# Attention of a two-layer decoder: the negative maximum and first exponential of a row group ahead of the filling work, one score chunk in a transposition bank, and a head's reciprocals turned one block later

## The chip, the cores and the metric

The kernel runs on one core of a Trainium2 chip. The metric is the device time of one execution in microseconds (us), and lower is better. Every time below is in us unless ns is written.

## The reference

The program is a two-layer decoder trunk on 2048 tokens of width 1024: a Mamba-2 layer, then multi-head latent attention whose keys and values come from a shared latent, then a final RMS norm. The change touches the attention alone. It has 16 heads, queries and keys of 64 + 32 channels, values of 64, and a causal mask:

```python
def causal_block_attention(q_nope, q_rope, k_nope, k_rope, v):
    for i in range(S // Q_BLOCK):
        ...
        s = (q_nope @ k_nope + q_rope @ k_rope) * scale
        p = softmax(where(mask, s, -inf))
        outs.append(p @ v[:, :kv_len])
```

The softmax's division is done later here: the exponentials go into the product with v undivided, their row sums are kept, and the reciprocals multiply the gate in the last stage (`back`).

## The kernel before

**Stages.** `mamba`, `mla` (projections), `heads` (attention, from about 2008 us of the profiled execution to 2908) and `back` (output projection, gate, norm). Only `heads` is written differently after the change.

**Tiling of the attention.** For each of 16 heads there are four query blocks (0 to 3) of 512 rows, each of four row groups of 128 rows. The scores of a row group are cut into chunks of at most 512 keys: one chunk in block 0, two in block 1, three in block 2, four in block 3 (`cuts`). In this text

- **S b.j.n** is the score chunk n of row group j in block b: three matmuls (lines 88 to 90), and for the group's last chunk a fourth that adds the mask (L1220). It fills one PSUM bank. The banks are eight: four with the tag `mm`, four with the tag `tr`. Scores take `mm` banks in rotation, so that the fifth chunk waits until the first one's exponential has read its bank.
- **M b.j.n** is the row maximum of the chunk, a reduction on VectorE (L1221), **N b.j** the negative maximum over the group's chunks, `nm` (L1225, VectorE), and **E b.j.n** the exponential on ScalarE (L1233), which needs N b.j, writes `Pr` and sums its rows into `sm`. L1237 reduces `sm` into the head's `sums`.
- **T b.k** turns key tile k of a block's exponentials: up to four transpositions (L1248) into one `tr` bank. **H b.k** (ScalarE, L119) and then **L b.k** (VectorE, L120) split the bank into two f16 halves `PTs`; after L the bank is free. **V b.k** multiplies both halves with the values (L1258, L1259) into the block's accumulator, which holds another `tr` bank during the block and is read by `Os` (ScalarE, L1265).
- **R** is the transposition of a head's 16 reciprocals (L1277); `rT` (ScalarE, L1279) reads it.

**Order.** TensorE's order is written out by hand. `scores` is a generator that yields after each chunk a word of T's and V's from the table `CREDIT`; the loop then issues that many turnings and products of blocks that are 20 chunks behind. This is the filling work: beside a head's block 2 the turnings of the head before's block 3 and of its own block 0 are issued, beside its block 3 those of its own blocks 1 and 2. In block 3 the last chunk of row group 0 is followed by `VVTTVTV`. The order of ScalarE and VectorE is made by a scheduler from the order in which the code emits its instructions. On all three engines it is the same in each head from 2 to 13, before the change and after it.

In the code before, the exponentials of a row group are put in a list `late` when the generator is called again, that is behind the filling work of the group's last chunk, and are issued one a chunk ahead of the next group's chunks:

```python
                    yield CREDIT[qb][j][n]
                nm = self.t(sp, "nm", [P, 1], bufs=4)
                v.tensor_reduce(nm, mx[:, :nb], AX.X, ALU.max, negate=True)
                ...
                late += [lambda n=n, f=exp: f(n) for n in range(nb)]
```

Queues: TensorE, ScalarE and VectorE each work in order. SyncE issues the stores of `Os` and `rT` and the loads of the output weights, GpSimd the other half of the stores and the loads of keys, values and queries. The loads of the output weights begin in head 13, and in heads 14 and 15 ScalarE converts them (`W<-wr` and `K<-wr`, L1331) between its attention work.

Of the kernel before, what the change touches and what calls it, by code (L numbers as in the profile page):

```python
# [21 lines left out]
P = 128  # L22
# [15 lines left out]
NP = 24  # L38
# [33 lines left out]
class Net:  # L72
# [1108 lines left out]
    def heads(self, sp):  # L1181
        nc, v = self.nc, self.nc.vector
        begun = []
        keys, vals, quer = self.keys, self.vals, self.quer

        def cuts(kv):

            out, at = [], 0
            while at < kv:
                w = min(TB, kv - at)  # L1190
                if kv - at == TB + P:
                    w = 384
                out.append((at, w))
                at += w
            return out

        def scores(h, qb, st):

            if h + 1 < NH:
                if qb == 2:  # L1200
                    self.load_k(h + 1, 0, NB)
                    self.load_v(h + 1)
                self.load_q(h + 1, qb)
            Q, K = quer.pop((h, qb)), keys[h]
            late = []
            for j in range(4):
                qs = slice(j * P, (j + 1) * P)
                parts = cuts(qb * TB + (j + 1) * P)
                nb = len(parts)
                mx = self.t(sp, "mx", [P, 4], bufs=4)  # L1210
                banks = []
                for n, (c0, w) in enumerate(parts):
                    if late:
                        late.pop(0)()
                    begun.append(0)
                    s = self.t(self.pp, "tr" if len(begun) <= 18 and len(begun) % 2 == 1 else "mm", [P, TB], bufs=4)
# [4 lines left out]
                    v.tensor_reduce(mx[:, n:n + 1], s[:, :w], AX.X, ALU.max)  # L1221
                    banks.append((s, w))
                    yield CREDIT[qb][j][n]
                nm = self.t(sp, "nm", [P, 1], bufs=4)
                v.tensor_reduce(nm, mx[:, :nb], AX.X, ALU.max, negate=True)  # L1225
                p = {}
                sm = self.t(sp, "sm", [P, 4], bufs=4)
                st["P"].append(p)

                def exp(n, j=j, nb=nb, parts=parts, banks=banks, nm=nm, p=p, sm=sm):  # L1230
                    s, w = banks[n]
                    x = self.t(sp, "Pr", [P, TB], bufs=NP)
                    nc.scalar.activation(x[:, :w], s[:, :w], AF.Exp, bias=nm, accum_out=sm[:, n:n + 1])  # L1233
                    for c in range(0, w, P):
                        p[(parts[n][0] + c) // P] = x[:, c:c + P]
                    if n == nb - 1:
                        v.tensor_reduce(sums[h][:, 4 * qb + j:4 * qb + j + 1], sm[:, :nb], AX.X, ALU.add)  # L1237

                late += [lambda n=n, f=exp: f(n) for n in range(nb)]
            for f in late:  # L1240
                f()

        def turn(h, qb, kb, st):

            jj = max(kb - 4 * qb, 0)
            pt = self.t(self.pp, "tr", [P, TB], bufs=4)
            for j in range(jj, 4):
                nc.tensor.transpose(pt[:, j * P:(j + 1) * P], st["P"][j][kb], self.ident)  # L1248
            c = slice(jj * P, TB)
            u = self.t(sp, "PTs", [P, 2, TB], F16, bufs=5)  # L1250
            self.pair16(u[:, 0, c], u[:, 1, c], pt[:, c], PSCALE)
            return u[:, :, c], c

        def values(h, qb, kb, st, u, c):
            if kb == 0:
                st["O"] = self.t(self.pp, "tr", [P, TB], bufs=4)
            nk = 4 * qb + 4
            nc.tensor.matmul(st["O"][:, c], vals[h][:, kb, :], u[:, 0], start=kb == 0, stop=False)  # L1258
            nc.tensor.matmul(st["O"][:, c], vals[h][:, kb, :], u[:, 1], start=False, stop=kb == nk - 1)  # L1259
            if kb == nk - 1:  # L1260
                finish(h, qb, st)

        def finish(h, qb, st):
            o = self.t(sp, "Os", [P, TB], bufs=3)
            nc.scalar.activation(o, st["O"], AF.Copy)  # L1265
# [36 lines left out]

        step = 0
# [206 lines left out]
```

## Time and profile before

| what | us |
|---|---|
| median of 3 runs (lowest, highest) | 3099.84 (3098.41, 3102.62) |
| the profiled execution's own time | 3099.32 |
| its span | 3097.2 |
| TensorE, VectorE, ScalarE, GpSimd busy | 2994.5, 2330.1, 1936.4, 615.3 |
| granted TensorE clock, mean | 0.995 of full speed |

The profile is of one execution, and the span is what its instructions cover. "Busy" of TensorE is from modelled ends: a 512-wide f16 matmul shows 0.38, while in a dense stretch the next one starts 0.216 after it, so matmuls overlap in the rows and a short wait between two of them is hidden by the overlap. Waits of TensorE are therefore counted below from start to start: what the distance exceeds the same distance in a dense stretch.

### The profile page before, as it was taken

To read this page: it belongs to the slowest core of one execution; us is meant where nothing else is said; L and a number is where in the kernel's file an instruction comes from. 1 tells how busy PE (TensorE), PEld (TensorE's weight loads), DVE (VectorE), ACT (ScalarE), POOL (GpSimd) and SP (SyncE) were. 2 spreads that over 40 slices of the span, in tenths; PEclk is the share of its full clock that TensorE was granted. 3 is DMA by queue.
4 is the path that set the end of the run, shared out by engine and by line. 5 is a ranking of instruction groups with operands and counts; after the bars stand their busy time and mean duration, and the time that the engine had idled before them with its cause. 6 is when DMAs were issued, how large, how long until landed. Compare 5 with 4: busy or idle time off the path is not lost.

```text
span 3097.2 us, 51355 instructions
## 1 busy us (share of the span) xinstructions
PE 2994.5 (97%) x17758; PEld 1759.2 (57%) x17758; DVE 2330.1 (75%) x5306; ACT 1936.4 (63%) x4920; POOL 615.3 (20%) x842
## 2 busy tenths in 40 slices
PE   7899999999999999999999999999999999999998
PEld 3466655555455554545555555456666666665777
DVE  7789887777777687797755453488888888888576
ACT  8777566665667656565534333388888888888422
POOL 0211122211222112222111212322122222222100
PEclk9999999999999999999999999999999999999999
DMA  8675436445454466364466555622223222232485
GB/s 298 221 235 181 151 106 220 129 158 163 153 191 162 131 207 222 121 199 145 145 214 197 194 173 170 197 49 60 55 56 67 54 58 57 54 88 75 130 261 158
DMA packets 205065, 457.11 MB, mean 148 GB/s; under 512 B 28114, under 2 KB 57554, under 8 KB 203364
## 3 DMA queue, kind: packets, MB, share of 16 engines
q1 hardware_dynamic: 176948, 375.94, 37.9%
q0 software_dynamic: 27856, 77.89, 9.8%
q8 instruction: 140, 2.29, 0.3%
q14 instruction: 121, 0.99, 0.1%
HBM read 340.99 MB, written 112.73 MB: 146 GB/s over the span
## 4 chain that ended last, share of the span: by engine, by line
PE 40%; DVE 5%; ACT 4%; issue 3%; DMA 2%; POOL 0%; SPq 0%; ACTq 0%; POOLq 0%; DVEq 0%
PE mm L88 7%; PE mm L90 6%; PE mm L89 6%; PE tr L1248 6%; PE tr L1259 3%; PE tr L1258 3%; PE tr L88 3%; PE tr L90 3%; PE tr L89 3%; ACT Pr L1233 2%; DVE PTs L120 1%; DMA os<-ri_d 1%; ACT PTs L119 1%; DVE mx L1221 1%; PE mm L1220 0%
## 5 line engine op out<-in xcount | busy, mean ns | idle before, releaser
L120 DVE SCALAR_TENSOR_TENSOR PTs<-tr,PTs 128x512 f16<-128x512 f32 (+3 forms) x640 | 374.2, 606 | 76.8 <-ACT PTs L119 69.7
L1233 ACT ACTIVATE Pr<-mm,nm 128x512 f32<-128x512 f32 (+2 forms) x631 | 394.2, 635 | 49.4 <-DVE nm L1225 44.9
L1221 DVE TENSOR_REDUCE mx<-mm 128x1 f32<-128x512 f32 (+2 forms) x631 | 373.1, 604 | 31.1 <-PE mm L90 28.3
L119 ACT ACTIVATE PTs<-tr 128x512 f16<-128x512 f32 (+3 forms) x640 | 329.4, 544 | 97.9 <-PE tr L1248 95.9
L1248 PE MATMUL tr<-pack,Pr 128*128 128x128 f32 x2176 | 317.5, 273 | 1.8 <-ACT Os L1265 1.4
L88 PE MATMUL mm<-xT,wsp 128*128 128x512 f16 x800 | 305.7, 382 | 7.9 <-ACT wsp L119 4.9
L89 PE MATMUL mm<-xT,wsp 128*128 128x512 f16 x800 | 304.6, 381 | 0.0
L90 PE MATMUL mm<-xT,wsp 128*128 128x512 f16 x800 | 303.6, 380 | 0.0
L1248 PEld LDWEIGHTS tr<-pack,Pr 128*128 128x128 f32 x2176 | 253.2, 141 | 68.9 <-ACT Os L1265 2.2
L88 PE MATMUL mm<-K,xT 96*128 96x512 f16 (+2 forms) x639 | 222.4, 348 | 27.5 <-ACT Pr L1233 24.0
L88 PE MATMUL mm<-wsp,xT 128*128 128x512 f16 (+1 forms) x640 | 232.0, 363 | 4.3 <-ACT craw L610 4.1
L89 PE MATMUL mm<-wsp,xT 128*128 128x512 f16 (+1 forms) x640 | 232.3, 363 | 3.0 <-DVE wsp L120 3.0
L89 PEld LDWEIGHTS <-xT 128*128 128x128 f16 (+1 forms) x1408 | 138.0, 98 | 168.1 <-issue 69.6
L616 DVE SCALAR_TENSOR_TENSOR cacc<-craw,pack,cacc 128x512 f32<-128x512 f32 x288 | 219.3, 790 | 18.0 <-ACT cacc L614 17.2
L90 PE MATMUL mm<-wsp,xT 128*128 128x512 f16 (+1 forms) x640 | 232.5, 364 | 0.0
L90 PE MATMUL mm<-K,xT 96*128 96x512 f16 (+2 forms) x639 | 221.8, 347 | 0.0
L89 PE MATMUL mm<-K,xT 96*128 96x512 f16 (+2 forms) x639 | 221.2, 346 | 0.0
L1258 PE MATMUL tr<-PTs,xT 128*128 128x512 f16 (+3 forms) x640 | 221.0, 347 | 0.1
L1259 PE MATMUL tr<-PTs,xT 128*128 128x512 f16 (+3 forms) x640 | 219.1, 347 | 0.0
L90 PEld LDWEIGHTS <-xT 128*128 128x128 f16 (+1 forms) x1408 | 136.9, 97 | 133.1 <-issue 5.7
L88 PEld LDWEIGHTS <-xT 128*128 128x128 f16 (+1 forms) x1408 | 137.7, 98 | 120.1 <-issue 8.5
L88 PE MATMUL mm<-wsp,yT 128*128 128x512 f16 (+1 forms) x512 | 197.4, 385 | 0.9 <-DVE sz L640 0.5
(456 smaller groups left out, 6795.8 us busy)
## 6 DMA issues: line engine op xcount, KB each, us to landing
wsp<-wi_d SPq DMA_DIRECT2D x96, 512.0 KB, 3.6
big<-cumT SPq DMA_DIRECT2D x64, 512.0 KB, 4.8
wraw<-in_ssm_w_out_dram SPq DMA_DIRECT2D x96, 256.0 KB, 3.6
wi_d<-wsp SPq DMA_DIRECT2D x32, 512.0 KB, 3.8
wsp<-wo_d SPq DMA_DIRECT2D x32, 512.0 KB, 3.5
wsp<-wu_d SPq DMA_DIRECT2D x28, 512.0 KB, 3.8
hx<-in_ssm_w_in_dram SPq DMA_DIRECT2D x48, 256.0 KB, 4.8
wraw<-in_ssm_w_in_dram SPq DMA_DIRECT2D x48, 256.0 KB, 4.4
```

The costliest lines, as they stand in the source:

```text
L88: mm(out, l_hi, r_hi, start=start, stop=False)
L89: mm(out, l_hi, r_lo, start=False, stop=False)
L90: mm(out, l_lo, r_hi, start=False, stop=stop)
L119: self.nc.scalar.activation(hi, src, AF.Copy, scale=scale)
L120: self.nc.vector.scalar_tensor_tensor(lo, src, scale, hi, ALU.mult, ALU.subtract)
L616: nc.vector.scalar_tensor_tensor(acc, raw[:, k:k + TB], wk[k], acc, ALU.mult, ALU.add)
L1221: v.tensor_reduce(mx[:, n:n + 1], s[:, :w], AX.X, ALU.max)
L1233: nc.scalar.activation(x[:, :w], s[:, :w], AF.Exp, bias=nm, accum_out=sm[:, n:n + 1])
L1248: nc.tensor.transpose(pt[:, j * P:(j + 1) * P], st["P"][j][kb], self.ident)
L1258: nc.tensor.matmul(st["O"][:, c], vals[h][:, kb, :], u[:, 0], start=kb == 0, stop=False)
L1259: nc.tensor.matmul(st["O"][:, c], vals[h][:, kb, :], u[:, 1], start=False, stop=kb == nk - 1)
```

## The change

Five things are written differently.

1. N is computed as soon as the group's last maximum is there, ahead of the yield. Where a group has one chunk (block 0), the maximum is written negated, and N as an instruction of its own is gone.
2. In blocks 2 and 3 (`nb > 2`) the group's first exponential is emitted ahead of the yield too.
3. S 3.1.0 of every head goes into a `tr` bank.
4. The row sums: in block 0 the exponential adds straight into `sums`; in the other blocks one reduction a block (over 4 groups and their chunks) replaces four.
5. A head's reciprocals are computed as before, but R, `rT` and the store to `ri_d` come at the end of the next head's block 0. The last head's stay where they were.

```diff
-            late = []
+            late, total = [], sums[h][:, 4 * qb:4 * qb + 4]
+            sm = self.t(sp, "sm", [P, 4, 4], bufs=2) if qb else total.unsqueeze(2)
...
-                    s = self.t(self.pp, "tr" if len(begun) <= 18 and len(begun) % 2 == 1 else "mm", [P, TB], bufs=4)
+                    spare = (qb, j, n) == (NB - 1, 1, 0) or len(begun) <= 18 and len(begun) % 2 == 1
+                    s = self.t(self.pp, "tr" if spare else "mm", [P, TB], bufs=4)
...
-                    v.tensor_reduce(mx[:, n:n + 1], s[:, :w], AX.X, ALU.max)
                     banks.append((s, w))
+                    if nb == 1:
+                        v.tensor_reduce(nm, s[:, :w], AX.X, ALU.max, negate=True)
+                    else:
+                        v.tensor_reduce(mx[:, n:n + 1], s[:, :w], AX.X, ALU.max)
+                    if n == nb - 1:
+                        if nb > 1:
+                            v.tensor_reduce(nm, mx[:, :nb], AX.X, ALU.max, negate=True)
+
+                        def exp(n, j=j, nb=nb, parts=parts, banks=banks, nm=nm, p=p):
+                            s, w = banks[n]
+                            x = self.t(sp, "Pr", [P, TB], bufs=NP)
+                            nc.scalar.activation(x[:, :w], s[:, :w], AF.Exp, bias=nm, accum_out=sm[:, j, n:n + 1])
...
+                            if j == 3 and n == nb - 1 and nb > 1:
+                                v.tensor_reduce(total, sm[:, :, :nb], AX.X, ALU.add)
+
+                        late += [lambda n=n, f=exp: f(n) for n in range(nb)]
+                        if nb > 2:
+                            late.pop(0)()
                     yield CREDIT[qb][j][n]
-                nm = self.t(sp, "nm", [P, 1], bufs=4)
-                v.tensor_reduce(nm, mx[:, :nb], AX.X, ALU.max, negate=True)
...
                 v.tensor_scalar(ri, ri, 0.5, None, ALU.mult)
+                inverse.append((h, ri))
+            if inverse and (qb == 0 or h == NH - 1):
+                h, ri = inverse.pop()
                 ps = self.t(self.pp, "tr", [P, TB], bufs=4)
                 nc.tensor.transpose(ps[:16, 0:P], ri, self.ident)
```

**Where instructions stand: VectorE in head 3, around the last maximum of row group 0 in block 3.** `mm_4791` and `mm_4742` are the bank of S 3.0.3 before and after, `nm_4800` and `nm_4736` are N 3.0, and the three lines of `PTs` are L 1.2, L 1.3 and L 1.4. Before:

```order
L1221 TENSOR_REDUCE mx_4785_24370<-mm_4791_24394 128x1
L120 SCALAR_TENSOR_TENSOR PTs_4794_24413<-tr_4793_24408,PTs_4794_24413 128x512
L120 SCALAR_TENSOR_TENSOR PTs_4796_24421<-tr_4795_24416,PTs_4796_24421 128x512
L1225 TENSOR_REDUCE nm_4800_24437<-mx_4785_24370 128x1
L120 SCALAR_TENSOR_TENSOR PTs_4799_24432<-tr_4798_24427,PTs_4799_24432 128x512
```

After:

```order
L1229 TENSOR_REDUCE mx_4735_24252<-mm_4742_24277 128x1
L1232 TENSOR_REDUCE nm_4736_24253<-mx_4735_24252 128x1
L120 SCALAR_TENSOR_TENSOR PTs_4748_24304<-tr_4747_24299,PTs_4748_24304 128x512
L120 SCALAR_TENSOR_TENSOR PTs_4750_24312<-tr_4749_24307,PTs_4750_24312 128x512
L120 SCALAR_TENSOR_TENSOR PTs_4753_24323<-tr_4752_24318,PTs_4753_24323 128x512
```

N 3.0 has moved ahead of L 1.2 and L 1.3.

**ScalarE at the same place.** The `PTs` lines are H 1.2, H 1.3, H 1.4 and H 1.5, the `Pr` lines E 3.0.0 to E 3.0.3. Before:

```order
L1265 ACTIVATE Os_4792_24404<-tr_4778_24351 128x512
L119 ACTIVATE PTs_4794_24413<-tr_4793_24408 128x512
L119 ACTIVATE PTs_4796_24421<-tr_4795_24416 128x512
L119 ACTIVATE PTs_4799_24432<-tr_4798_24427 128x512
L1233 ACTIVATE Pr_4803_24441,sm_4801_24439<-mm_4786_24371,nm_4800_24437 128x512
L1233 ACTIVATE Pr_4807_24455,sm_4801_24439<-mm_4789_24384,nm_4800_24437 128x512
L1233 ACTIVATE Pr_4809_24464,sm_4801_24439<-mm_4790_24389,nm_4800_24437 128x384
L1233 ACTIVATE Pr_4811_24471,sm_4801_24439<-mm_4791_24394,nm_4800_24437 128x256
L119 ACTIVATE PTs_4806_24452<-tr_4805_24448 128x384
```

After:

```order
L1272 ACTIVATE Os_4744_24290<-tr_4730_24237 128x512
L1289 ACTIVATE rT_4746_24296<-tr_4745_24294 16x128
L119 ACTIVATE PTs_4748_24304<-tr_4747_24299 128x512
L1237 ACTIVATE Pr_4743_24284,sm_4734_24251<-mm_4737_24254,nm_4736_24253 128x512
L119 ACTIVATE PTs_4750_24312<-tr_4749_24307 128x512
L119 ACTIVATE PTs_4753_24323<-tr_4752_24318 128x512
L1237 ACTIVATE Pr_4756_24330,sm_4734_24251<-mm_4740_24267,nm_4736_24253 128x512
L1237 ACTIVATE Pr_4760_24344,sm_4734_24251<-mm_4741_24272,nm_4736_24253 128x384
L119 ACTIVATE PTs_4759_24341<-tr_4758_24337 128x384
L1237 ACTIVATE Pr_4762_24353,sm_4734_24251<-mm_4742_24277,nm_4736_24253 128x256
```

E 3.0.0 stands two H's earlier, ahead of H 1.3 and H 1.4; `rT` has come in ahead of H 1.2. Of the other first exponentials of blocks 1 to 3, E 2.1.0 and E 2.2.0 have each moved ahead of one H (H 3.14 of the head before, and H 0.1); E 1.3.0, E 2.0.0, E 2.3.0, E 3.1.0, E 3.2.0 and E 3.3.0 follow the same instruction as before.

**VectorE half a block earlier, after the last maximum of row group 3 in block 2.** `mm_4775` and `mm_4726` hold S 2.3.2, `nm_4779` and `nm_4715` are N 2.3, the `PTs` line is L 1.0. Before:

```order
L1221 TENSOR_REDUCE mx_4761_24294<-mm_4775_24337 128x1
L1237 TENSOR_REDUCE sum_4639_23868<-sm_4760_24293 128x1
L1225 TENSOR_REDUCE nm_4779_24356<-mx_4761_24294 128x1
L120 SCALAR_TENSOR_TENSOR PTs_4777_24348<-tr_4776_24343,PTs_4777_24348 128x512
L1221 TENSOR_REDUCE mx_4785_24370<-mm_4786_24371 128x1
```

After:

```order
L1229 TENSOR_REDUCE mx_4714_24184<-mm_4726_24220 128x1
L120 SCALAR_TENSOR_TENSOR PTs_4729_24234<-tr_4728_24229,PTs_4729_24234 128x512
L1232 TENSOR_REDUCE nm_4715_24185<-mx_4714_24184 128x1
L1229 TENSOR_REDUCE mx_4735_24252<-mm_4737_24254 128x1
L1229 TENSOR_REDUCE mx_4735_24252<-mm_4740_24267 128x1
```

Here N has moved the other way: it stands behind L 1.0.

TensorE's order is the same but for R, which stands behind V 0.3 instead of behind V 3.15. The banks differ. In the built program S 3.1.0 takes the `tr` bank of T 1.2, one `tr` bank holds the accumulator, and until E 3.1.0 has read S 3.1.0 the turnings have two: T 1.5 takes the bank of T 1.3, T 2.0 that of T 1.6, and T 2.1 that of T 1.7. Before, T 1.5 took the bank of T 1.2 and T 2.0 that of T 1.5. The `mm` banks rotate without S 3.1.0, so S 3.1.1 waits for E 3.0.0, S 3.1.2 for E 3.0.1, S 3.1.3 for E 3.0.2 and S 3.2.0 for E 3.0.3; elsewhere a chunk waits, as before, for the exponential of the fourth chunk before it.

More of the change, by code (lines that the diff above doesn't have):

```diff
@@ L1209, in scores @@
                 nb = len(parts)
-                mx = self.t(sp, "mx", [P, 4], bufs=4)
+                mx, nm = (self.t(sp, m, [P, n], bufs=4) for m, n in (("mx", 4), ("nm", 1)))
+                p = {}
+                st["P"].append(p)
                 banks = []
@@ L1289, in ahead @@
                 yield from scores(h, qb, states[n])
+        inverse = []
         units = [(h, qb, kb, states[n]) for n, (h, qb) in enumerate(jobs) for kb in range(4 * qb + 4)]
```

14 lines of the change are left out of this document (2 added, 12 removed).

## The prediction

> **What bounds the kernel now.** I read the page first, then the attention in stretches, then who waits for whom, then the order of time at the places where TensorE waits.
>
> ```profile
> span 3097.2 us, 51355 instructions
> PE 2994.5 (97%) x17758; PEld 1759.2 (57%) x17758; DVE 2330.1 (75%) x5306; ACT 1936.4 (63%) x4920; POOL 615.3 (20%) x842
> L88 PE MATMUL mm<-K,xT 96*128 96x512 f16 (+2 forms) x639 | 222.4, 348 | 27.5 <-ACT Pr L1233 24.0
> ```
>
> TensorE sets the time. Of its idle time that an edit in the attention can touch, the last row has nearly all: the first matmul of a score chunk (L88 with K) waits for an exponential, that is for a bank. The stretches are the attention's start, one head (from one S 2.0.2 to the next), twelve heads, and the end:
>
> ```profile
> 2010.00:2068.72 58.72, 54.51 (x353) 34.74 (x351) 50.45 (x134) 48.30 (x139) 13.39 (x22) 1.00 0.27 60
> 2124.35:2179.98 55.63, 54.18 (x353) 35.35 (x353) 47.50 (x114) 45.30 (x126) 12.16 (x19) 1.00 0.28 58
> 2068.72:2736.32 667.60, 650.13 (x4237) 424.20 (x4237) 570.05 (x1368) 543.66 (x1501) 145.87 (x228) 1.00 0.28 58
> 2736.32:2910.00 173.68, 165.95 (x1064) 108.88 (x1064) 142.41 (x327) 142.52 (x372) 39.22 (x38) 1.00 0.28 67
> ```
>
> The columns are length, busy time of TensorE, its weight loads, VectorE, ScalarE and GpSimd, then clock and DMA. A head takes 55.63, twelve take 667.60 = 12 x 55.63, so the loop is periodic. The row shows 1.45 of idle TensorE a head. Counted from start to start it is 2.85, in eleven places: S 0.2.0 0.12, S 2.0.2 0.29, S 2.1.1 0.22, S 2.2.1 0.14, R 0.14, S 3.0.3 0.10, S 3.1.0 1.37, S 3.2.0 0.23, S 3.2.1 0.07, S 3.3.1 0.09, S 3.3.2 0.08. VectorE and ScalarE have 8 to 10 us a head to spare, so only their order and delay count. Here is the largest wait, in head 3 (start, length, engine; in the brackets idle time and who ended it):
>
> ```profile
> 2197.07 1.04 PE L1248 MATMUL tr<-pack,Pr 128*128 128x128 f32 x8
> 2199.03 0.38 PE L1259 MATMUL tr<-PTs,xT 128*128 128x512 f16 x1
> 2200.62 0.38 PE L88 MATMUL mm<-K,xT 96*128 96x512 f16 x1 [1.21 <-ACT Pr L1233]
> ...
> 2197.77 1.08 ACT L119 ACTIVATE PTs<-tr 128x512 f16<-128x512 f32 x2
> 2199.08 0.60 ACT L119 ACTIVATE PTs<-tr 128x512 f16<-128x512 f32 x1 [0.22 <-PE tr L1248]
> 2199.79 0.69 ACT L1233 ACTIVATE Pr<-mm,nm 128x512 f32<-128x512 f32 x1
> 2200.47 0.68 ACT L1233 ACTIVATE Pr<-mm,nm 128x512 f32<-128x512 f32 x1
> ...
> 2197.43 0.88 DVE L1221 TENSOR_REDUCE mx<-mm 128x1 f32<-128x384 f32 x2
> 2198.40 1.29 DVE L120 SCALAR_TENSOR_TENSOR PTs<-tr,PTs 128x512 f16<-128x512 f32 x2
> 2199.61 0.15 DVE L1225 TENSOR_REDUCE nm<-mx 128x1 f32<-128x4 f32 x1
> 2199.71 0.69 DVE L120 SCALAR_TENSOR_TENSOR PTs<-tr,PTs 128x512 f16<-128x512 f32 x1
> ```
>
> S 3.1.0 could start at 2199.25 (V 1.1's second matmul + 0.22). It starts 0.14 after E 3.0.0's end (2199.79 + 0.69). E waits for N 3.0, and N stands behind L 1.2 and L 1.3 though its last maximum ended at 2198.31.
>
> **The change, part by part.** From these rows: an E of 512 holds ScalarE 0.68, an H 0.48 to 0.5 (ends after 0.60), an L holds VectorE 0.60 (ends after 0.69), N 0.10; H starts 0.70 after its T, L 0.03 after its H, E 0.03 after its N. TensorE needs 0.44 for a full T, 0.43 for a V, 0.645 for an S of 512.
>
> Small reductions:
>
> ```profile
> L1225 DVE TENSOR_REDUCE nm<-mx 128x1 f32<-128x1 f32 x64 | 9.5, 148 | 1.0
> L1237 DVE TENSOR_REDUCE sum<-sm 128x1 f32<-128x2 f32 x64 | 9.7, 152 | 14.4 <-ACT Pr L1233 12.0
> ```
>
> 64 N's (9.5) and 256 - 48 = 208 sums (x 0.15 = 31) leave VectorE. The wider sum is not in the trace: no less than 0.15, and no more than the 0.42 that a reduction of 128x256 takes; I take 0.16, since 16 columns are nearest to the first. None of it is on TensorE's path, because VectorE is idle 8 us a head; it counts as 0, and the cover is that idle time.
>
> Block 2. N 1.3 moves ahead of L 3.7 and L 3.8:
>
> ```profile
> 2177.18 0.68 DVE L1221 TENSOR_REDUCE mx<-mm 128x1 f32<-128x512 f32 x1
> 2177.78 1.28 DVE L120 SCALAR_TENSOR_TENSOR PTs<-tr,PTs 128x512 f16<-128x512 f32 x2
> 2178.97 0.14 DVE L1225 TENSOR_REDUCE nm<-mx 128x1 f32<-128x2 f32 x1
> 2179.15 0.69 ACT L1233 ACTIVATE Pr<-mm,nm 128x512 f32<-128x512 f32 x1 [1.18 <-DVE nm L1225]
> 2179.98 0.27 PE L88 MATMUL mm<-K,xT 96*128 96x256 f16 x1
> ```
>
> E 1.3.0 then starts near 2177.9 and its bank is free at 2178.75, 0.9 ahead of S 2.0.2's turn: 0.29 gone. The same 1.2 of lead carries on down ScalarE and VectorE and takes the 0.22 and the 0.14 with it (my margins there are 0.28 and 0.20). R's wait of 0.14 goes as R goes, with its 0.11 of work. Against it, E 2.2.1 now stands behind H 0.1, and S 2.3.2 waits about 0.09 for it. Block 2 gains 0.29 + 0.22 + 0.14 + 0.14 - 0.09 = 0.70, and T 1.0 comes 0.70 + 0.11 = 0.81 earlier.
>
> Start of block 3. This is where I expect the gain of block 2 to go. N 2.3 has moved behind L 1.0:
>
> ```profile
> 2192.83 0.61 PE L1248 MATMUL tr<-pack,Pr 128*128 128x128 f32 x4
> 2195.12 0.38 PE L88 MATMUL mm<-K,xT 96*128 96x512 f16 x1
> 2193.53 0.60 ACT L119 ACTIVATE PTs<-tr 128x512 f16<-128x512 f32 x1
> 2194.19 0.69 ACT L1233 ACTIVATE Pr<-mm,nm 128x512 f32<-128x512 f32 x1
> 2194.00 0.16 DVE L1225 TENSOR_REDUCE nm<-mx 128x1 f32<-128x3 f32 x1
> 2194.16 0.69 DVE L120 SCALAR_TENSOR_TENSOR PTs<-tr,PTs 128x512 f16<-128x512 f32 x1
> ```
>
> After: T 1.0 at 2192.0, H 1.0 2192.7 to 2193.3, L 1.0 from 2193.4 (VectorE is on M 2.3.2 until then), N 2.3 at 2194.0, E 2.3.0 2194.2 to 2194.9, and S 3.0.1, which needs its bank, at 2195.05. Its turn is at 2194.3, so it waits 0.75. S 3.0.3 needs E 2.3.2: 2194.2 + 3 x 0.68 + 0.14 = 2196.4, as before (2196.36). The 0.81 is given back whole. R's 0.11 now comes here, behind V 0.3, so T 1.2 starts 0.15 later than before.
>
> Row groups 0 and 1 of block 3. T 1.2 at 2197.2, rT and H 1.2 to 2198.5, E 3.0.0 from 2198.4. S 3.1.0 needs no `mm` bank but T 1.2's, free after L 1.2 at 2199.25; its turn is then 2199.4 or later: 1.37 gone. Of S 3.2.0 to S 3.3.2 the waits 0.23, 0.07, 0.09, 0.08 go too, but for about 0.10 at S 3.3.1 (E 3.2.1 keeps its place behind H 2.4): 0.37. New waits come from the turnings, which are down to two banks. T 1.5 needs L 1.3: from T 1.2 on that is 0.70 + 0.48 (H 1.2) + 0.66 (E 3.0.0, now ahead) + 0.60 + 0.03 + 0.69 + 0.06 = 3.2, while TensorE has 2.8 of work there: 0.41. T 2.0 needs L 1.6:
>
> ```profile
> 2204.14 0.49 PE L1248 MATMUL tr<-pack,Pr 128*128 128x128 f32 x3
> 2204.90 0.60 PE L1248 MATMUL tr<-pack,Pr 128*128 128x128 f32 x4
> 2204.62 0.38 ACT L119 ACTIVATE PTs<-tr 128x256 f16<-128x256 f32 x1 [1.98 <-PE tr L1248]
> 2205.03 0.42 DVE L120 SCALAR_TENSOR_TENSOR PTs<-tr,PTs 128x256 f16<-128x256 f32 x1 [0.30 <-ACT PTs L119]
> ```
>
> T 1.6 starts at 2204.14 and L 1.6 ends at 2205.45, 1.31 later, + 0.06 = 1.37; T 2.0 starts after 0.76. So 0.61. (The 0.06 from L's end to T is bounded by the 0.03 from H to L and the 0.14 from E to S.) Sum: 1.37 + 0.37 - 0.41 - 0.61 = 0.72, less 0.15 = 0.57 a head. S 0.2.0's 0.12 stays, its chain starts at a T and is not touched.
>
> Those T rows meet a rule of the Trainium skill, "Perfetto Trace Analysis", Matmuls: independent matmul groups should rotate through different PSUM banks, so that one group's evacuation overlaps the next one's matmuls. It speaks against taking a bank from the turnings, and the row with 1.37 against 0.76 agrees; the page gives no size. Without what the rule fears, the 0.41 and 0.61 would not come, the sum would be 1.59 a head and the time near 3077.
>
> Ends. Head 0 has a wait of its own at S 3.1.0, 1.92 in the row, 2.08 from start to start:
>
> ```profile
> 2033.72 0.38 PE L88 MATMUL mm<-K,xT 96*128 96x512 f16 x1 [1.92 <-ACT Pr L1233]
> 2811.98 0.33 PE L1248 MATMUL tr<-pack,Pr 128*128 128x128 f32 x1 [1.38 <-ACT Os L1265]
> ```
>
> There 2.08 + 0.37 - 0.61 - some 0.3 = 1.5. What VectorE saves in the first chunks is lost at S 3.0.1 in the way shown. In head 14 the second row's wait is for `Os`, behind a weight conversion: it stays, and T 2.0 gets L 1.6 behind two more conversions, which eats that head's gain. I count 0.5 for heads 14 and 15 together. Stores and loads on SP and GpSimd move with the heads; the store of the reciprocals comes 6 us later for heads 0 to 14, and the last stage waits for head 15's in any case: 0.
>
> Sum: 13 x 0.57 + 1.5 + 0.5 = 9.4. The profiled execution's own time is 3099.32 (2.1 over its span), which gives 3089.9; the median is 0.5 above it, so 3090.4.
>
> **The rivals.**
> 1. All bank waits go, and neither the turnings' two banks nor N 2.3 behind L 1.0 costs anything, because ScalarE and VectorE run further ahead than I reckon. For it: 8 to 10 us of slack a head. Against: both new waits are chains from one T, in which nothing is slack. 2.85 - 0.12 = 2.73 x 14 + 2 = 40, 3060. The same page's section Optimization Strategy, that the same gap repeating can mean too little PSUM, would read the 1.21 so.
> 2. The new waits eat the rest: if H 1.2, behind `Os` and `rT`, is 0.3 later than I have it, then E 3.0.0, H 1.3, L 1.3 and T 1.5 are too, and 14 x 0.3 = 4 goes, leaving 5: 3095. At 0.6, 3099. It is within the bound from 0.23 on. For it: L 1.1 and the block sum now stand close to each other ahead of N 3.0.
> 3. Slower: the turnings become the bound. If H 1.6 waits until E 3.0.3 and E 3.1.0 are done, T 2.0 waits 1.1 more, 0.5 a head net loss: + 8, 3107. Against: E 3.0.3 ends near 2202.1 and H 1.6 can start at 2203.8, so ScalarE would have to be 1.7 later.
> 4. That the scheduler undoes the change is partly so already (N 2.3) and in the sum.
>
> **How the numbers follow.** A measurement tells 0.2% (6.2 us) from no change. Forecast, between 6.2 and 16 faster: 0.57. Rival 1 or a good part of it: 0.09. Rival 2, within 0.2%: 0.28. Rival 3 or another loss over 0.2%: 0.06. The range takes in the sum without the turnings' waits (3077) and the new waits at their worst short of rival 3 (3100): 3078 to 3100. Faster 0.66, same 0.28, slower 0.06.
>
> **What the profile after would show.** A head's period of 55.1 instead of 55.63. No wait of L88 for `Pr` near S 2.0.2 and S 3.1.0, a new one of about 0.75 at S 3.0.1; waits of L1255 (the transposition's new line) for L120 at T 1.5 and T 2.0 of 0.3 to 0.6; VectorE about 2.4 less a head; R without a wait behind V 0.3. I am wrong if N 2.3 is ready before L 1.0 frees VectorE all the same, if T 2.0 starts without a wait, or if ScalarE reaches E 3.0.0 much later than 2198.4 on this head's clock.

## The result and the profile after

| | before | after |
|---|---|---|
| median (us) | 3100.23 | 3095.93 |
| ratio to before, 95% interval | | 0.9983 [0.9977, 0.9989] |
| profiled execution: own time, span | 3099.32, 3097.2 | 3088.58, 3086.6 |
| head period in the trace | 55.63 | 55.36 |

The change makes the kernel 5.3 us faster (0.0017 x 3100; by the interval 3.4 to 7.1). The forecast was 9.4. The way was right, the size 0.56 of what was said, and the point lies inside the 0.2% that the text called "no change". Of the 22 executions of each kernel one took over twice as long (6321.87 and 7862.99 us); it is left out of the ratio and of the 21 spoken of below.

The two profiled executions differ by twice as much, 10.6 us of span, and the first thing to read is where. These are stretches of the changed kernel, then of the one before: ahead of the attention, start and head 0, twelve heads, the rest of the attention, `back`. (Columns as in the prediction: length, busy time by engine, clock, DMA.)

```profile
0.00:2003.29 2003.29, 1941.90 (x11346) 1048.96 (x11346) 1449.40 (x3245) 1162.42 (x2835) 417.85 (x553) 1.00 0.55 180
2003.29:2062.23 58.94, 56.39 (x369) 35.91 (x367) 49.78 (x110) 49.78 (x143) 14.15 (x23) 1.00 0.30 69
2062.23:2726.84 664.61, 649.12 (x4237) 422.25 (x4236) 556.50 (x1165) 539.46 (x1501) 145.86 (x228) 1.00 0.28 58
2726.84:2897.40 170.56, 163.71 (x1056) 106.64 (x1054) 139.16 (x286) 140.14 (x368) 39.12 (x38) 1.00 0.28 67
2897.40:3086.61 189.21, 178.24 (x760) 141.79 (x758) 115.68 (x230) 40.91 (x76) 0.82 (x1) 0.98 0.75 218
```

```profile
0.00:2007.98 2007.98, 1946.38 (x11346) 1050.32 (x11347) 1449.86 (x3245) 1161.10 (x2835) 415.25 (x553) 0.99 0.55 180
2007.98:2068.72 60.74, 56.53 (x369) 36.04 (x367) 51.72 (x136) 48.99 (x140) 14.14 (x23) 1.00 0.29 68
2736.32:2907.78 171.46, 163.73 (x1054) 107.09 (x1054) 142.41 (x327) 141.85 (x371) 39.22 (x38) 1.00 0.28 67
2907.78:3097.24 189.46, 177.69 (x759) 141.52 (x758) 116.09 (x230) 40.84 (x76) 0.82 (x1) 0.98 0.73 218
```

Ahead of the attention both programs are the same, with the same number of instructions on each engine (one weight load aside), and yet 4.7 us lie there (2007.98 - 2003.29). They belong to the execution: the profiled one of after is the fastest of its 21 (3088.58 to 3102.02), with a mean clock of 0.997 where their mean is 0.994. Head 0 gives 1.80, the twelve heads 667.60 - 664.61 = 2.99, the rest of the attention 0.90: 5.7 in the attention, which agrees with the ratio.

What TensorE waits for in it has changed. From the page of the changed kernel (compare the row of L88 in the prediction, with 27.5 of idle time):

```profile
L1255 PE MATMUL tr<-pack,Pr 128*128 128x128 f32 x2176 | 322.2, 274 | 11.7 <-DVE PTs L120 10.7
L88 PE MATMUL mm<-K,xT 96*128 96x512 f16 (+4 forms) x623 | 216.6, 348 | 12.3 <-ACT Pr L1237 11.9
```

The waits for an exponential have halved, and the turnings, which waited 1.8 in all before, now wait 11.7, nearly all for an L. Head 3 shows the three largest. First S 3.0.1 (T 1.1 is the first row of PE):

```profile
2187.31 0.60 PE L1255 MATMUL tr<-pack,Pr 128*128 128x128 f32 x4
...
2188.47 0.38 PE L88 MATMUL mm<-K,xT 96*128 96x512 f16 x1 [0.56 <-ACT Pr L1237]
...
2186.87 0.68 DVE L120 SCALAR_TENSOR_TENSOR PTs<-tr,PTs 128x512 f16<-128x512 f32 x1
2187.47 0.15 DVE L1232 TENSOR_REDUCE nm<-mx 128x1 f32<-128x3 f32 x1
...
2187.65 0.69 ACT L1237 ACTIVATE Pr<-mm,nm 128x512 f32<-128x512 f32 x1 [0.88 <-DVE nm L1232]
```

N 2.3 stands behind L 1.0 (2186.87), E 2.3.0 waits 0.88 for it, and S 3.0.1 starts 0.13 after E's end: 0.73 from start to start. Then T 2.0:

```profile
2196.80 0.49 PE L1255 MATMUL tr<-pack,Pr 128*128 128x128 f32 x3
...
2197.70 0.62 DVE L120 SCALAR_TENSOR_TENSOR PTs<-tr,PTs 128x256 f16<-128x256 f32 x2 [0.30 <-ACT PTs L119]
...
2198.18 0.33 PE L1255 MATMUL tr<-pack,Pr 128*128 128x128 f32 x1 [0.45 <-DVE PTs L120]
```

It starts 1.38 after T 1.6, 0.06 after the end of L 1.6 (2198.12, the first of the two L's in the row): 0.68. And T 3.0, of which nothing was said:

```profile
2213.22 0.53 ACT L119 ACTIVATE PTs<-tr 128x384 f16<-128x384 f32 x1
...
2213.61 0.25 DVE L1281 RECIPROCAL ri<-sum 128x16 f32<-128x16 f32 x1
2213.78 0.50 DVE L1227 TENSOR_REDUCE nm<-mm 128x1 f32<-128x384 f32 x1
2214.19 1.14 DVE L120 SCALAR_TENSOR_TENSOR PTs<-tr,PTs 128x384 f16<-128x384 f32 x3
...
2214.88 0.63 PE L1255 MATMUL tr<-pack,Pr 128*128 128x128 f32 x4 [0.17 <-DVE PTs L120]
```

H 2.9 ends at 2213.75, but L 2.9 (first of the three) starts at 2214.19, because VectorE takes the maximum of the next head's S 0.2.0 (L1227) first; T 3.0 needs L 2.9's bank and loses 0.36.

Counted as in the prediction, from start to start, a middle head of each kernel below waits as follows (median of heads 3 to 11; "S 2" is all of block 2's chunks and so on; the period is from one R to the next).

| kernel | ratio [interval] | period | S 0 | S 2 | R | S 3.0.1 | S 3.0.3 | T 1.3 | T 1.5 | S 3.1 | T 2.0 | S 3.2, 3.3 | T 3.0 | sum |
|---|---|---|---|---|---|---|---|---|---|---|---|---|---|---|
| before | 1 | 55.63 | .12 | .65 | .13 | 0 | .10 | 0 | 0 | 1.37 | 0 | .47 | 0 | 2.84 |
| after | 0.9983 [0.9977, 0.9989] | 55.36 | .12 | 0 | 0 | .73 | .18 | .25 | .22 | 0 | .68 | 0 | .36 | 2.54 |
| N 2.3 first | 0.9956 [0.9942, 0.9969] | 54.79 | .12 | 0 | 0 | .26 | .18 | .36 | 0 | 0 | .67 | 0 | .36 | 1.96 |
| old bank | 0.9963 [0.9950, 0.9975] | 55.01 | .12 | 0 | 0 | .72 | .18 | .25 | 0 | .26 | 0 | .30 | .36 | 2.19 |
| both orders | 0.9928 [0.9914, 0.9941] | 54.43 | .12 | 0 | 0 | .26 | .18 | .36 | 0 | 0 | .67 | 0 | 0 | 1.59 |
| both orders, old bank | 0.9938 [0.9926, 0.9951] | 54.50 | .12 | 0 | 0 | .26 | .18 | .36 | 0 | .46 | 0 | .30 | 0 | 1.69 |
| parts 1, 2 alone | 0.9956 [0.9944, 0.9968] | 54.83 | .12 | .06 | .16 | 0 | .11 | 0 | 0 | 1.15 | 0 | .48 | 0 | 2.08 |
| parts 1, 2, 4 | 0.9979 [0.9969, 0.9988] | 55.30 | .12 | 0 | .52 | 0 | 0 | 0 | 0 | 1.15 | 0 | .30 | .36 | 2.45 |
| part 3 alone | 1.0059 [1.0047, 1.0071] | 56.91 | .12 | 1.21 | .13 | 0 | .11 | 0 | 0 | .39 | .67 | 1.14 | .35 | 4.12 |
| without part 5 | 0.9938 [0.9926, 0.9950] | 54.73 | .12 | 0 | .53 | 0 | 0 | 0 | 0 | .17 | .68 | .03 | .36 | 1.88 |
| orders, R at block 1 | 0.9921 [0.9908, 0.9933] | 54.22 | .29 | 0 | 0 | .25 | .18 | 0 | 0 | 0 | .67 | 0 | 0 | 1.40 |
| the same, old bank | 0.9936 [0.9924, 0.9949] | 54.33 | .29 | 0 | 0 | .25 | .18 | 0 | 0 | .51 | 0 | .30 | 0 | 1.53 |

Period less sum is 52.75 to 52.85 in all twelve: the sum of waits is what the period follows.

### The profile page after: what moved, and what is told of

Same layout as the page of the kernel before. It is cut to its first block, busy times and chain, and to the rows that moved or that the text cites. A ratio compares the mean times of both kernels' runs of the same rounds, so it can differ in the third digit from the quotient of the medians.

```text
span 3086.6 us, 51064 instructions
## 1 busy us (share of the span) xinstructions
PE 2989.3 (97%) x17758; PEld 1755.6 (57%) x17758; DVE 2310.5 (75%) x5034; ACT 1932.7 (63%) x4920; POOL 617.8 (20%) x842
## 4 chain that ended last, share of the span: by engine, by line
PE 38%; DVE 6%; ACT 4%; issue 3%; DMA 2%; POOL 0%; SPq 0%; ACTq 0%; POOLq 0%; DVEq 0%
PE tr L1255 6%; PE mm L88 6%; PE mm L90 6%; PE mm L89 6%; PE tr L88 3%; PE tr L90 3%; PE tr L89 3%; PE tr L1265 3%; PE tr L1266 3%; ACT Pr L1237 2%; DVE PTs L120 1%; ACT PTs L119 1%; DVE mx L1229 1%; DMA os<-ri_d 1%; DMA wr<-in_mla_w_out_dram 0%
## 5 line engine op out<-in xcount | busy, mean ns | idle before, releaser
L1237 ACT ACTIVATE Pr<-mm,nm 128x512 f32<-128x512 f32 (+3 forms) x615 | 386.1, 636 | 21.7 <-DVE nm L1232 21.5
L1229 DVE TENSOR_REDUCE mx<-mm 128x1 f32<-128x512 f32 (+2 forms) x553 | 327.3, 615 | 26.0 <-PE mm L90 21.9
L1255 PE MATMUL tr<-pack,Pr 128*128 128x128 f32 x2176 | 322.2, 274 | 11.7 <-DVE PTs L120 10.7
L88 PE MATMUL mm<-xT,wsp 128*128 128x512 f16 x800 | 305.9, 382 | 7.4 <-ACT wsp L119 4.5
L88 PE MATMUL mm<-wsp,xT 128*128 128x512 f16 (+1 forms) x640 | 230.3, 361 | 4.1 <-ACT craw L610 4.0
L88 PE MATMUL mm<-K,xT 96*128 96x512 f16 (+4 forms) x623 | 216.6, 348 | 12.3 <-ACT Pr L1237 11.9
L90 PE MATMUL mm<-K,xT 96*128 96x512 f16 (+4 forms) x623 | 215.7, 346 | 0.0
L89 PE MATMUL mm<-K,xT 96*128 96x512 f16 (+4 forms) x623 | 215.2, 345 | 0.0
L88 PEld LDWEIGHTS <-xT 128*128 128x128 f16 (+1 forms) x1408 | 137.2, 97 | 119.1 <-issue 6.9
L88 PE MATMUL mm<-wsp,yT 128*128 128x512 f16 (+1 forms) x512 | 197.4, 385 | 2.6 <-DVE sz L640 2.2
```

The costliest lines, as they stand in the source:

```text
L88: mm(out, l_hi, r_hi, start=start, stop=False)
L89: mm(out, l_hi, r_lo, start=False, stop=False)
L90: mm(out, l_lo, r_hi, start=False, stop=stop)
```

## The experiments

**N 2.3 ahead of L 1.0.** L 1.0 of each head is tied behind N 2.3 on VectorE.

```diff
-                            v.tensor_reduce(nm, mx[:, :nb], AX.X, ALU.max, negate=True)
+                            self.nm = v.tensor_reduce(nm, mx[:, :nb], AX.X, ALU.max, negate=True)
...
-            self.pair16(u[:, 0, c], u[:, 1, c], pt[:, c], PSCALE)
+            with self.tc.issue_after(self.nm.ins) if (qb, kb) == (1, 0) else ExitStack():
+                self.pair16(u[:, 0, c], u[:, 1, c], pt[:, c], PSCALE)
```

> The changed kernel with one VectorE order altered: L 1.0 of every head is made to follow N 2.3. (The scheduler answers with H 1.3 ahead of E 3.0.0.) Theory A, that N 2.3 behind L 1.0 gives back what block 2 gained: the 0.73 us a head at S 3.0.1 goes, and with it the 0.25 at T 1.3 (H 1.1 stands behind the late E 2.3.n) and most of the 0.22 at T 1.5. T 2.0's 0.67 and T 3.0's 0.36 stay. Head period 55.36 - 1.1 = 54.3, time 3100 - 5 - 15 x 1.1 = 3079, ratio to before 0.993. Rival B, the time at S 3.0.1 is bound by ScalarE's and VectorE's work as such: the wait only moves on to S 3.0.3 and S 3.1.n; period 55.2 to 55.4, ratio 0.997 to 0.999.

Measured: ratio 0.9956, period 54.79. In this kernel's head 3 N comes first, E 2.3.0 waits for it 0.42 and not 0.88, and S 3.0.1 starts without idle time in the row:

```profile
2187.51 0.15 DVE L1232 TENSOR_REDUCE nm<-mx 128x1 f32<-128x3 f32 x1
2187.59 0.68 DVE L120 SCALAR_TENSOR_TENSOR PTs<-tr,PTs 128x512 f16<-128x512 f32 x1
...
2187.70 0.69 ACT L1237 ACTIVATE Pr<-mm,nm 128x512 f32<-128x512 f32 x1 [0.42 <-DVE nm L1232]
2188.53 0.38 PE L88 MATMUL mm<-K,xT 96*128 96x512 f16 x1
```

One place in VectorE's order is worth 0.57 a head, twice what the whole change gained in a middle head. Theory A had 1.1: S 3.0.1 falls as it said (0.26 are left), T 1.5's wait goes, but T 1.3's does not go, it grows to 0.36. That part of A is wrong: in this kernel T 1.3 starts 0.05 after the end of `Os` and 0.23 after that of L 1.1, so it is not a late H 1.1 that it waits for (see R behind block 1).

**The bank given back.** S 3.1.0 of the changed kernel in an `mm` bank.

```diff
-                    spare = (qb, j, n) == (NB - 1, 1, 0) or len(begun) <= 18 and len(begun) % 2 == 1
+                    spare = len(begun) <= 18 and len(begun) % 2 == 1
```

> The changed kernel with S 3.1.0 back in an mm bank, all else kept. Theory A, that early N and E alone have removed the 1.37 us and the tr bank only costs: E 3.0.0 ends 0.54 ahead of S 3.1.0's turn, so S 3.1.0 does not wait; T 2.0's 0.67 and T 1.5's 0.22 go; some 0.3 comes at S 3.2.0, which now needs E 3.1.0. Period 54.8, time 3100 - 5 - 14 x 0.6 = 3087, ratio 0.9955. Rival B, that the bank is what removed the 1.37: S 3.1.0 waits again by 0.5 to 1.4, period 55.4 to 56, ratio 0.998 to 1.002.

Measured: 0.9963, period 55.01: faster than with the bank. S 3.1.0, the place of the 1.37, does not wait, as E 3.0.0 ends 0.54 before it (E 3.0.0 and S 3.1.0 in head 3):

```profile
2194.44 0.66 ACT L1237 ACTIVATE Pr<-mm,nm 128x512 f32<-128x512 f32 x1
...
2195.64 0.38 PE L88 MATMUL mm<-K,xT 96*128 96x512 f16 x1
```

So it is not the bank that removes the 1.37 in the changed kernel: E 3.0.0 stands ahead of H 1.3 and H 1.4 and ends in time without it. (Parts 1 and 2 do not bring E 3.0.0 there by themselves: see parts 1, 2 and 4.) In this kernel the bank costs 0.35 net: T 2.0 and T 1.5 (0.90) against S 3.1.1 and S 3.2 (0.56). Theory A, with 0.3 of these last and a period of 54.8, put them too low.

**Both orders.** As N 2.3 first, and the maximum of the next head's S 0.2.0 tied behind L 2.9 (`self.low`):

```diff
+                        with self.tc.issue_after(self.low.ins) if h and j == 2 else ExitStack():
+                            v.tensor_reduce(nm, s[:, :w], AX.X, ALU.max, negate=True)
```

> As the kernel with N 2.3 ahead of L 1.0, and beside it the maximum of S 0.2.0 of the next head made to follow L 2.9. Theory A: the 0.36 at T 3.0 goes as well, period 54.0, time 3074, ratio 0.9915. Rival B, that T 3.0 waits for H 2.9 or for ScalarE and not for VectorE's order: period as without this edit, 54.3 by theory A for N 2.3.

Measured: 0.9928, period 54.43: 0.36 less than with N 2.3 alone, and T 3.0's wait is gone, to the hundredth what it was. Two lines of VectorE's order make the change 4.2 times as good (0.72% against 0.17%).

**Both orders, old bank.**

> Both orders of VectorE altered and S 3.1.0 back in an mm bank. Theory A: of the 2.54 us of waits a head that the changed kernel has, S 0.2.0's 0.12 and some 0.3 at S 3.2.0 are left; period 53.3, time about 3100 - 5 - 14 x 2.1 = 3066, ratio 0.989. Rival B, waits take each other's place: no more than the best of the three single edits, ratio 0.993 or above. A third reading, that a denser TensorE is granted a lower clock and gives part of it back, would show a period of 53.3 but a mean clock below 0.994 and a ratio above 0.991.

Measured: 0.9938, period 54.50. Theory A's 53.3 fails: T 1.3 stays, and without the bank S 3.1.0 (0.28), S 3.1.1 (0.18) and S 3.2 (0.30) take T 2.0's place. With N 2.3 early, E 3.0.0 goes behind H 1.3 in the built order, and the bank is then worth 0.07, little more than the 0.04 by which the periods of two profiles of the kernel before differ (see below). The clock of the denser kernels is not lower: a mean of 0.9946 to 0.9948 over the runs of the two kernels with both orders, 0.9941 over those of the kernel before on the same chip. The third reading falls.

**Parts 1 and 2 alone**, in the kernel before.

> The kernel before with parts 1 and 2 of the change alone: N right behind the group's last maximum (block 0's negated maximum too), first exponential ahead of the filling work in blocks 2 and 3. Bank, sums and R as before. The scheduler then sets N 2.3 ahead of L 1.0, but E 3.0.0 stays behind H 1.3 and H 1.4. Theory A: block 2 gains 0.56 (0.70 without R's 0.14), S 3.0.1 waits some 0.25 and not 0.73, no wait comes at T 2.0, and S 3.1.0 keeps about 1.2 of its 1.37; period 54.9 to 55.1, ratio 0.9955 to 0.997, at least as good as the whole change. Rival B, that the bank is needed for the gain of block 2 to reach the head's end: period 55.5 to 55.7, ratio 0.9985 or above.

Measured: 0.9956, period 54.83, just under A's 54.9. Theory A holds in place (S 3.1.0 keeps 1.15). S 3.0.1, for which it had 0.25, does not wait at all. Of the 1.37, a late N 3.0 thus made 0.22: it now stands ahead of L 1.3, and E 3.0.0 waits for H 1.3 and H 1.4 alone. Two of the five parts, alone, gain 2.6 times what all five gain.

**Part 5 undone**: the changed kernel without the four lines with `inverse`, R at the end of its own head.

> The changed kernel with part 5 undone: a head's R and rT at its own end again. Theory A: R's move costs in two ways, its 0.11 with rT's 0.25 sits ahead of T 1.2 and H 1.2, and the scheduler's order with it has N 2.3 behind L 1.0; undone, N 2.3 stands ahead and the S 3.0.1 wait falls from 0.73 to 0.25, while R's old wait of 0.14 comes back and T 2.0's 0.67 and T 3.0's 0.36 stay. Period 54.9 to 55.0, ratio 0.996. Rival B, that the move of R is worth its 0.14 and nothing hangs on it otherwise: period 55.5, ratio 0.9985 to 1.000.

Measured: 0.9938, period 54.73, better than A's 54.9. In the changed kernel the late R cost 0.63 a head: with R in its old place the scheduler sets N 2.3 ahead of L 1.0 again, and S 3.0.1, S 3.0.3, T 1.3 and T 1.5 (1.38 in all) do not wait. What the move had saved was larger than thought too: R waits 0.53 in this order, not 0.14.

**Part 3 alone**: S 3.1.0's bank in the kernel before.

```diff
+                    spare = (qb, j, n) == (NB - 1, 1, 0) or len(begun) <= 18 and len(begun) % 2 == 1
+                    s = self.t(self.pp, "tr" if spare else "mm", [P, TB], bufs=4)
```

> The kernel before with part 3 alone: S 3.1.0 in a tr bank. Theory A: S 3.1.0's 1.37 goes, but the next chunk S 3.1.1 then needs E 3.0.0's bank, which ends as late as before, and waits about 0.3; T 2.0 waits 0.6 to 0.7; the block 2 waits stay. Net 0.3 to 0.5 a head, period 55.1 to 55.4, ratio 0.997 to 0.998. Rival B, that the wait only moves to S 3.1.1 and T 1.5 and T 2.0 add to it: period 55.6 to 56.2, ratio 1.000 or above.

Measured: 1.0059, period 56.91. Both theories miss, B by less. The bank does what was said at its place (the 1.37 at S 3.1.0 goes, S 3.1.1 waits 0.39, T 2.0 0.67), but every chunk behind it takes another bank, and the scheduler answers with other orders. The waits of block 2 rise from 0.65 to 1.21. In block 3, N 3.2 (L1226) now stands behind L 2.2 and E 3.2.0 behind H 2.3 and H 2.4, and S 3.3.0 waits 1.14:

```profile
2215.20 0.69 DVE L120 SCALAR_TENSOR_TENSOR PTs<-tr,PTs 128x512 f16<-128x512 f32 x1 [0.25 <-ACT PTs L119]
...
2215.81 0.15 DVE L1226 TENSOR_REDUCE nm<-mx 128x1 f32<-128x4 f32 x1
...
2215.38 1.09 ACT L119 ACTIVATE PTs<-tr 128x512 f16<-128x512 f32 x2 [0.21 <-PE tr L1249]
...
2216.35 0.69 ACT L1234 ACTIVATE Pr<-mm,nm 128x512 f32<-128x512 f32 x1
...
2217.19 0.38 PE L88 MATMUL mm<-K,xT 96*128 96x512 f16 x1 [0.98 <-ACT Pr L1234]
```

That is the pattern of the 1.37, moved two row groups on. N 3.2 is there at 2215.96, but E 3.2.0 starts at 2216.35, when ScalarE has taken both H's: what is late is E's place, more than N. Here one bank more moved the wait and did not remove it.

**The kernel before, once more.**

> The kernel before, unchanged, as a measure of what two identical programs differ by and which mean clocks they are granted. Every theory: ratio 1.000 with an interval that holds 1. If a denser TensorE is granted a lower clock, its clocks lie above those of the changed kernel (0.993 to 0.997, median 0.994); if not, they are the same.

Measured: 0.9997 [0.9987, 1.0006], clock 0.9938 on average (the kernel before beside it 0.9935). The period in its trace is 55.67, 0.04 more than in the first profile: that is what two profiles of one program differ by.

**Parts 1, 2 and 4.**

> Parts 1, 2 and 4 of the change: the kernel with early N and E and old bank and R, and with the row sums merged as well. In the built order the merged sums leave VectorE's order with the maximum of S 0.2.0 of the next head ahead of L 2.9, where the kernel with parts 1 and 2 alone has L 2.9 first. Theory A, that the 0.36 us at T 3.0 come from part 4 by way of that order: T 3.0 waits 0.3 to 0.4 a head, the rest as with parts 1 and 2, period 54.83 + 0.36 = 55.1 to 55.2, ratio 0.9965 to 0.998. Rival B, that the sums cost or bring nothing and T 3.0 waits because of the bank or R: period 54.8, ratio 0.9956.

Measured: 0.9979, period 55.30 against 54.83 with parts 1 and 2. The sums cost 0.47 a head, and theory A has the place. Here are the reciprocal, the next maximum and L 2.9 on VectorE, and T 3.0, with parts 1 and 2:

```profile
2218.25 0.25 DVE L1280 RECIPROCAL ri<-sum 128x16 f32<-128x16 f32 x1
2218.44 0.56 DVE L120 SCALAR_TENSOR_TENSOR PTs<-tr,PTs 128x384 f16<-128x384 f32 x1
...
2218.97 0.55 DVE L1226 TENSOR_REDUCE nm<-mm 128x1 f32<-128x384 f32 x1
...
2219.20 0.60 PE L1254 MATMUL tr<-pack,Pr 128*128 128x128 f32 x4
```

and with part 4 as well:

```profile
2216.66 0.25 DVE L1281 RECIPROCAL ri<-sum 128x16 f32<-128x16 f32 x1
2216.83 0.49 DVE L1227 TENSOR_REDUCE nm<-mm 128x1 f32<-128x384 f32 x1
2217.24 1.13 DVE L120 SCALAR_TENSOR_TENSOR PTs<-tr,PTs 128x384 f16<-128x384 f32 x3
...
2217.93 0.63 PE L1255 MATMUL tr<-pack,Pr 128*128 128x128 f32 x4 [0.17 <-DVE PTs L120]
```

Fewer instructions on VectorE, and the one that TensorE waits for comes later. R's wait rises by 0.36 as well (E 2.2.0 goes ahead of H 0.1 in this order), and the small waits at S 2, S 3.0.3 and S 3.3 go (0.34), so that the 0.47 is not wholly made up of the places: the sum of waits has 0.37.

This kernel also shows what the bank and the late R do to each other. It differs from the one without part 5 by the bank (part 3) alone, and from the one with the old bank by the late R (part 5) alone. With parts 1, 2 and 4 in all of them, the periods are 55.30 with neither, 54.73 with the bank, 55.01 with the late R and 55.36 with both: each gains by itself (0.57 and 0.29), and together they lose 0.06. S 3.1.0 tells why. Here are H 1.2 and H 1.3, N 3.0, H 1.4, E 3.0.0 and S 3.1.0 of the kernel with neither:

```profile
2194.10 1.09 ACT L119 ACTIVATE PTs<-tr 128x512 f16<-128x512 f32 x2
...
2195.34 0.14 DVE L1232 TENSOR_REDUCE nm<-mx 128x1 f32<-128x4 f32 x1
...
2195.41 0.60 ACT L119 ACTIVATE PTs<-tr 128x512 f16<-128x512 f32 x1 [0.22 <-PE tr L1255]
2195.90 0.68 ACT L1237 ACTIVATE Pr<-mm,nm 128x512 f32<-128x512 f32 x1
...
2196.72 0.38 PE L88 MATMUL mm<-K,xT 96*128 96x512 f16 x1 [0.98 <-ACT Pr L1237]
```

N 3.0 ends at 2195.48, but E 3.0.0 stands behind H 1.4 and starts at 2195.90, and S 3.1.0 loses 1.15. A bank of its own spares S 3.1.0 this wait. With the late R the scheduler sets E 3.0.0 ahead of H 1.3 and H 1.4 instead, and then the bank has nothing left to remove there and only takes from the turnings.

**R behind block 1**, in the kernel with both orders.

```diff
-            if inverse and (qb == 0 or h == NH - 1):
+            if inverse and (qb == 1 or (h, qb) == (NH - 1, NB - 1)):
```

> The changed kernel with both VectorE orders altered (N 2.3 ahead of L 1.0, L 2.9 ahead of S 0.2.0's maximum), and R issued at the end of the next head's block 1 and not of its block 0. Theory A, that T 1.3's 0.36 comes from R holding a tr bank just when the accumulator's changes hands: behind V 1.7 the banks are slack, T 1.3's wait goes and none comes; left are T 2.0 0.67, S 3.0.1 0.25, S 3.0.3 0.18, S 0.2.0 0.12; period 54.43 - 0.36 = 54.05, ratio to before 0.992. Rival B, that T 1.3 waits for H 1.1 and L 1.1 whatever R does, or that R's wait appears behind V 1.7: period 54.4, ratio 0.993.

Measured: 0.9921, period 54.22. T 1.3's 0.36 is gone, so it came from R: R took a bank at the moment when `Os` was to free the accumulator's (in the kernel with both orders T 1.3 starts 0.05 after `Os` ends). In its place S 0.1.0 waits 0.17, which theory A did not have; 0.21 is the net.

**The same, old bank.**

> As the kernel with both orders and R behind block 1, with S 3.1.0 in an mm bank. Theory A, that with early exponentials the bank is a wash: T 2.0's 0.67 goes, and 0.28 at S 3.1.0, 0.18 at S 3.1.1, 0.06 at S 3.2.0, 0.24 at S 3.2.1 come; period within 0.15 of the one with the bank, 54.05 to 54.2. Rival B, that the bank pays once nothing else waits: at least 0.3 a head better with it, period 54.35 or more here.

Measured: 0.9936, period 54.33: the bank is worth 0.11 a head here, by theory A's bound a wash. The medians differ by more, 5.1 us, and so do the granted clocks: 0.9952 on average with the bank, 0.9942 without.

**Two turnings in one bank**, in the kernel with R behind block 1. The last two turnings of each block have two transpositions and one; they share a bank, an H and an L.

```diff
+            if kb == 4 * qb + 3:
+                return half.pop()
...
+            if jj == 2:
+                nc.tensor.transpose(pt[:, P:2 * P], st["P"][3][kb + 1], self.ident)
-            c = slice(jj * P, TB)
+            c = slice((1 if jj == 2 else jj) * P, TB)
...
+            if jj == 2:
+                half.append((u[:, :, P:2 * P], slice(3 * P, TB)))
+                return u[:, :, 2 * P:], slice(2 * P, TB)
```

> As the kernel with both orders and R behind block 1 (S 3.1.0 in a tr bank), and the last two turnings of each block share one tr bank and one H and L (the one transposition of the last goes to columns 128 to 255 of the bank of the one before). Theory A, that T 2.0 waits because T 1.6 and T 1.7 hold both banks: T 2.0's 0.67 goes (it takes the bank of T 1.5, free since L 1.5), period 53.4, time some 10 below the kernel without the sharing, ratio 0.989. Rival B, that the wait moves on to T 2.1, which then needs the bank of the pair, or to S 3.1.1 and S 3.2.0, whose exponentials are bound by ScalarE: period 53.9 to 54.1, ratio 0.991 to 0.992.

Measured: 0.9901 [0.9885, 0.9916], median 3066.19, the best of all; period 53.99. Who TensorE waited for between 2120 and 2722, in the changed kernel, in the one with R behind block 1, and in this one (in all, times, longest; waits hidden by overlapping rows are missing):

```profile
PE tr L1255 <- DVE PTs L120: 7.2, 23, 0.5
PE mm L88 <- ACT Pr L1237: 6.2, 11, 0.6
```

```profile
PE tr L1256 <- DVE PTs L120: 5.0, 11, 0.5
```

```profile
PE mm L88 <- ACT Pr L1238: 2.0, 11, 0.2
```

T 2.0's wait is gone, as theory A says, and 0.52 of its 0.67 comes back at S 3.1.1 (0.17) and S 3.2.1 (0.35), much as rival B says. S 0.2.0's 0.12 goes too, S 3.0.1 waits 0.06 less and S 2.2.2 0.10 more: 0.23 a head is kept.

## Why the prediction was right, and where it was off

**Block 2: right.** S 2.0.2, S 2.1.1, S 2.2.1 and R do not wait. The 0.09 at S 2.3.2 did not come.

**N 2.3 behind L 1.0: right in place and size**, 0.75 forecast, 0.73 measured; with N 2.3 first, the period falls by 0.57. This step is shown. What stood behind it was not seen: it is part 5 that puts N there. (In the three kernels with parts 1 and 2 and without part 5, N 2.3 stands ahead of L 1.0.)

**S 3.1.0's 1.37: gone, for another reason than given.** The text had the `tr` bank remove it. Without the bank it is gone as well. The text's own figures say so: E 3.0.0 from 2198.4 frees an `mm` bank by 2198.4 + 0.68 + 0.14 = 2199.2, and S 3.1.0's turn was put at 2199.4. The sum charges the bank's price (0.41 and 0.61) for a gain that E 3.0.0's place ahead of two H's gives alone; in this kernel the bank costs 0.35 net.

**The turnings on two banks: right.** T 2.0 0.61 forecast, 0.68 measured; T 1.5 0.41 against 0.22 (T 1.3, ahead of it, waits 0.25, which comes off what T 1.5 has to wait). Both go when the bank is given back. The waits of S 3.2 and S 3.3 go (the 0.10 at S 3.3.1 did not stay).

**The step that failed is part 4, "none of it is on TensorE's path ... it counts as 0".** It measured 0.47 a head beside parts 1 and 2. Its visible piece, 0.36 at T 3.0, stands in the changed kernel too, and is more than the gap between forecast and result (0.57 - 0.27 = 0.30). That part 4 makes it there as well is not shown: the changed kernel without part 4 was not run, and part 3 alone gives 0.35 at T 3.0, with the same maximum ahead of L 2.9. Idle VectorE time was named as the cover, but the cover must lie at the place. The working followed the new order at N 2.3 and N 3.0 and not at the head's seam, where L 2.9 had changed places with a maximum. The other misses nearly cancel: T 1.3 0.25 where the text had 0.15 at T 1.2 (R's own 0.11 in it), S 3.0.3 +0.08, T 2.0 +0.07, against T 1.5 -0.19, S 3.3.1 -0.10, S 2.3.2 -0.09. That they cancel is luck.

**Ends: right.** Head 0 1.8 against 1.5; the stretch from head 13's block 2 to the end 0.9, against 0.57 + 0.5.

**The rivals.** Rival 1 (all waits go) is far off. Rival 2 (the new waits eat the rest, 3095 to 3099) gives the measured time, but for a reason that did not come: it has H 1.2 and E 3.0.0 later than reckoned, while E 3.0.0 starts 1.22 after T 1.2 (2191.86 and 2190.64), where the text had 1.2, and T 1.5, its place, waited less than forecast. Its time came by another road, T 3.0. Rival 3 did not happen here; part 3 alone shows that a loss of that size was near, though mostly by late exponentials. Of the text's own classes, that of 0.28 came (within 0.2%), not that of 0.66.

**VectorE's saving: wrong.** The forecast was 2.4 less a head; the twelve heads show (570.05 - 556.50) / 12 = 1.13, with 17 instructions fewer: 66 ns each, where the rows say 147 to 155. Nothing hung on it.

**The rules of the Trainium skill.** "Perfetto Trace Analysis", Matmuls, that matmul groups should rotate through different banks, agrees with T 2.0's 0.67, which goes when the turnings have their bank. Its section Optimization Strategy, that a gap which repeats can mean too little PSUM, is half of the story here: the 1.37 repeated in every head, and one bank more made the kernel before 0.59% slower, while with parts 1, 2 and 4 in place the same bank gains 0.57 a head. Without any bank, parts 1 and 2 remove 0.22 of the wait where E 3.0.0 stays behind H 1.3 and H 1.4, and all of it where E 3.0.0 stands ahead of them.

## What to carry to other kernels

Where a scheduler makes the order of an engine, an edit's price is in the new order: compare it at every place where the bounding engine takes a result, also for the edits that "cost nothing", because taking instructions away reorders the others. Follow a repeated wait for a buffer back to the queue that frees it before giving it a buffer: here the causes were an exponential behind two instructions that it did not need and a small reduction behind a long instruction, and tying two instructions in front of their neighbours gave three times what the five edits gave. Do not price an edit alone: the bank gained 0.57 a head without the late R and cost 0.35 with it. Where two profiles are compared, subtract first what lies in stretches that the edit did not touch; here that was 4.7 of 10.6 us.

## What the runs showed of the hardware

Small reductions on VectorE (128x1 from 1 to 4 columns) show 147 to 155 ns in their rows and add some 66 ns to its busy time, since they overlap their neighbours (N 2.3 at 2187.51 above shows 0.15, and L 1.0 starts 0.08 after it). The Trainium skill, "Perfetto Trace Analysis", Optimizing Scalar/DVE Operations, gives a VectorE instruction on SBUF an overhead of about 60 ns of engine time and a profiled latency of about twice that, and the traces agree.

One program's runs on one core lie 13.4 us apart (3088.58 to 3102.02), and their granted clocks 0.993 to 0.997; the slower ones have the lower clock (correlation -0.68 over 21 runs). Two single executions can thus differ by 0.43% with nothing changed; the head period, at a clock of 1.00, differed by 0.04 of 55.63, under 0.1%, between two profiles of the kernel before.
